# A gated feed-forward's down-projection: one engine's order stays written out, another's is handed to the scheduler

## The chip, the cores and the metric

The kernel runs on one core of a Trainium2 chip. Its five engines each take instructions from a queue of their own and keep its order: TensorE (PE) multiplies matrices into PSUM, VectorE (DVE) and ScalarE (ACT) work on tiles, GpSimd (POOL) does a little elementwise work and issues some stores, SyncE (SP) issues most DMAs. An instruction that waits for a semaphore holds back all that stands behind it on its engine. The metric is the device time of one launch in microseconds (us); times of a kernel are medians over its runs.

## The reference

One layer of a streaming encoder over 2048 prompt rows and 64 sample rows of width 1024. The last of its three sub-layers is the one that matters here:

```
def conv_ffn(xn, ff_buf, w_up, ffn_conv_w, w_down):
    up, ff_new = causal_dwconv(xn @ w_up, ff_buf, ffn_conv_w)
    a, g = jnp.split(up, 2, axis=-1)
    return (jax.nn.gelu(g) * a) @ w_down, ff_new
...
    y, ff_new = conv_ffn(rms_norm(x, p['norm_ffn_pre']), ff_buf, p['w_up'], p['ffn_conv_w'], p['w_down'])
    x = x + rms_norm(y, p['norm_ffn_post'])
```

`w_down` is 2816 by 1024, so the product sums over 22 blocks of 128. Everything is in float32, and the kernel splits each operand into a high and a low part and adds three products, so that the matrix engine keeps float32 accuracy.

## The kernel before, in words

Phases 1 to 3 do the token mixing and the cross-attention. Phase 4 (`phase4`) does the up-projection, the convolution and the gate, in three passes over the rows with 22 blocks each, and stores the gated rows, `da`, to the DRAM tile `hd` from POOL's queue (L1491 and after). Phase 5 (`phase5`) is the down-projection.

Phase 5 sums over the 22 blocks in six parts of 3, 3, 4, 4, 4 and 4 blocks (`PARTS`, L37). Each part goes through nine groups of rows: eight of 256 rows and one of the 64 sample rows (`groups`, `work`; the small group is last in part 0 and first in the others). In a list `work` of 54 items, item i is one part and one group:

- `load_down` loads a part's weights, 512 KB a block, into `raw` (three buffers, shared with phase 4's weights) and splits them: ACT casts the high part `dh` (L103), DVE subtracts to get the low part `dl` (L104). Two pools of weights alternate by part, so part p+2 overwrites those of part p.
- `load_h` loads a group's gated rows into `hr` (two buffers) and splits them the same way into the high and low half of `hh` (two buffers).
- For each 128 rows and each half of the 1024 columns, PE does three matmuls per block (L117 to L119; L128 and L129 for the small group) into a PSUM tile `y`, of which there are eight. In part 0 ACT copies it to the sum `acc`, later DVE adds it (L1589).
- In the last part `post` (L553) finishes each 128 rows: ACT squares (L560), POOL multiplies by the gain `gpost` (L564), DVE combines the statistics (L565, L95), POOL takes the power (L97), and `finish` (L570, DVE) multiplies and adds the residual row `xt` (two buffers). It then has SP store the two halves as `out_y`. `finish` of one tile is called within `post` of the next one.

What sets the order: PE and SP have been under a manual order since the start of phase 3 (L1058; the stack `self.ms` closes after phase 5), so on these two the instructions stand as the code issues them. In the last part ACT, DVE and POOL are under a manual order too (L1565). Elsewhere a scheduler places instructions. So SP issues a group's `hr` where `need(i + 1)` stands in the loop: one item ahead of the one being multiplied, and in the last part behind the `xt` loads and `out_y` stores of the items before it.

```
need(i)
need(i + 1)
...
h = hs.pop(i)
```

Of the kernel before, what the change touches and what calls it, by code (L numbers as in the profile page):

```python
# [35 lines left out]
HEAD = 120  # L36
PARTS = [3, 3, 4, 4, 4, 4]  # L37
# [4 lines left out]
def tw(j):  # L42
    return P if j < 16 else NS_TOK
# [24 lines left out]
class Prog:  # L68
# [68 lines left out]
    def build(self):  # L137
        tc, nc = self.tc, self.nc
        with ExitStack() as es:
            cp = self.pool(es, "const")  # L140

            self.pool(es, "edge", side="right").pool.tile([P, 8], F32, name="edge")
            self.rawp = self.pool(es, "raw", side="right")
            self.ident = cp.tile([P, P], F32, name="ident")
            make_identity(nc, self.ident)
            self.ones = cp.tile([P, P], F32, name="ones")
            nc.vector.memset(self.ones, 1.0)
            sm = cp.tile([P, 16 + 2 * NT], F32, name="small")
            self.mhalf, self.bg = sm[:, 0:8], sm[:, 8:16]
            self.r_all, self.rk_all = sm[:, 16:16 + NT], sm[:, 16 + NT:]  # L150
            nc.vector.memset(self.mhalf, -0.5)
            self.cst = cp.tile([P, CST_W], F32, name="cst")
            self.dma(self.cst, self.a["cst"])
            self.dma(self.bg, self.a["bg"].partition_broadcast(P))
            self.G = cp.tile([P, NT, 8], F32, name="G")
            self.aT = cp.tile([P, NR], F32, name="aT")
            self.em = cp.tile([P, NR], F32, name="em")
            self.wsb = cp.tile([P, NR], F32, name="wsb")
            self.wcb = cp.tile([P, NR], F32, name="wcb")
            dt = tc.dram_tile  # L160
            self.yaT = dt([4, P, T], F32, name="yaT")
            self.x2T = dt([KT, P, T], F32, name="x2Td")
            self.hd = dt([NF, P, T], F32, name="hd")
            self.wsd = dt([NF, P, 4, D // 2], F32, name="wsd")
            self.qT = dt([4, P, T], F32, name="qTd")
            self.kvo = dt([T, KVO], F32, name="kvo")
            self.nmd = dt([NR, P], F32, name="nmd")
            self.wd = dt([NR, P], F32, name="wd")
            self.mkd = dt([KT, P, NM], F32, name="mkd")
            self.mvd = dt([KT, P, NM], F32, name="mvd")  # L170
            self.od = dt([P, KT, NS_TOK], F32, name="od")
            self.ys = dt([NS_TOK, D], F32, name="ysd")
            self.x1 = dt([T, D], F32, name="x1d")
            self.x2 = dt([T, D], F32, name="x2d")
            self.pe = mybir.EngineType.PE
            self.zes = es.enter_context(ExitStack())
            self.qes = es.enter_context(ExitStack())
            self.fl_es = ExitStack()
            self.fl = self.pool(self.fl_es, "fill", space=PSUM)
            self.phase1()  # L180
            self.phase2()
            with ExitStack() as self.ms:
                self.phase3()
                self.phase4()
                self.phase5()


    def phase1(self):
# [1319 lines left out]
    def phase5(self):  # L1508
        tc, nc, a = self.tc, self.nc, self.a
        V = nc.vector  # L1510
        with ExitStack() as es:
            ac0 = self.pool(es, "p5a")
            w0 = self.pool(es, "p5w")
            ac1 = self.pool(es, "p5b")
# [8 lines left out]
            def load_down(pi, f0, nf):  # L1523
                ws = []
                pool = w1 if pi % 2 else w0
                for i in range(nf):
                    raw = self.raw(a["w_down"][f0 + i])
                    wh = pool.tile([P, D], F32R, tag="h%d" % i, name="dh", bufs=1)
                    wl = pool.tile([P, D], F32R, tag="l%d" % i, name="dl", bufs=1)
                    self.split(wh, wl, raw)  # L1530
                    ws.append((wh, wl))
                return ws

            def load_h(f0, nf, t0):
                n = min(2 * P, T - t0)
                hr = ld.tile([P, 4, 2 * P], F32, tag="hr", name="hr", bufs=2)
                self.dma(hr[:, :nf, :n], self.hd[f0:f0 + nf, :, t0:t0 + n].rearrange("f p t -> p f t"))
                hh = ld.tile([P, 2, 4, 2 * P], F32R, tag="hh", name="hh", bufs=2)
                if n == 2 * P:
                    self.split(hh[:, 0, :nf], hh[:, 1, :nf], hr[:, :nf])  # L1540
                    return hh
                h2 = hh[:, 0, :, 0:P].rearrange("p f (two t) -> p f two t", two=2)
                self.split(h2[:, :nf, 0], h2[:, :nf, 1], hr[:, :nf, :n])
                return h2

            groups = [NP_TOK] + list(range(0, NP_TOK, 2 * P))
            f0s = [sum(PARTS[:i]) for i in range(len(PARTS))]
# [3 lines left out]
            def need(i):  # L1551
                if i < len(work) and i not in hs:
                    pi, t0 = work[i]
                    hs[i] = load_h(f0s[pi], PARTS[pi], t0)
            with tc.high_priority(offset=HEAD):
                need(0)
                ws = {0: load_down(0, 0, PARTS[0])}
            held = None
            tail = None
            for i, (pi, t0) in enumerate(work):  # L1560
                last = pi == len(PARTS) - 1
                if i == len(PARTS):
                    self.dma(gpost, a["g_ffnpost"].partition_broadcast(P))
                if last and tail is None:
                    tail = es.enter_context(tc.manual_schedule(engines={mybir.EngineType.Activation,  # L1565
                                                                        mybir.EngineType.DVE, mybir.EngineType.Pool})) or 1
                need(i)
                need(i + 1)
                if t0 == groups[3] and pi + 1 < len(PARTS):
                    ws[pi + 1] = load_down(pi + 1, f0s[pi + 1], PARTS[pi + 1])  # L1570
                h = hs.pop(i)
                for j in range(t0 // P, (t0 + min(2 * P, T - t0) + P - 1) // P):
                    w = tw(j)
                    s = j * P - t0
                    if last:
                        xt = ld.tile([P, D], F32, tag="xt", name="xt5", bufs=2)
                        self.dma(xt[:w], self.x2[j * P:j * P + w])
                    for nh in range(2):
                        sl = slice(nh * 512, (nh + 1) * 512)
                        pt = py.tile([P, 512], F32, tag="y", name="y5")  # L1580
                        if w == P:
                            self.mm3(pt, [(h[:, 0, q, s:s + P], h[:, 1, q, s:s + P], wh[:, sl], wl[:, sl])
                                          for q, (wh, wl) in enumerate(ws[pi])])
                        else:
                            self.mm2(pt, [(h[:, q], wh[:, sl], wl[:, sl]) for q, (wh, wl) in enumerate(ws[pi])])
                        if pi == 0:
                            nc.scalar.copy(acc[j][:, sl], pt)
                        else:
                            V.tensor_tensor(out=acc[j][:, sl], in0=pt, in1=acc[j][:, sl], op=ALU.add)  # L1589
                    if last:  # L1590
                        yv = acc[j]
                        if w < P:
                            fo = ev.tile([P, D], F32, name="fo5")
                            self.fold(fo[:w], yv)
                            yv = fo
                        f = self.post(ev, [yv[:w, 0:512], yv[:w, 512:D]], gpost, xt, self.o["y"][j * P:j * P + w], w=w,
                                      yn=yv, junk=junk, hold=held or (), pg=j != 15)
                        held = [f]
                if i and work[i - 1][0] != pi:
                    ws.pop(pi - 1, None)  # L1600
# [89 lines left out]
```

## Time and profile before

| | us |
|---|---|
| median of 3 runs | 2946.56 |
| lowest and highest run | 2938.88, 2947.24 |
| the profiled execution's own time | 2947.28 |
| its span, first to last instruction | 2945.6 |

The rows below are from the profiled execution. Its time less its span is 1.7 us, which lies around the instructions. Times in rows are us from the span's start unless marked ns; phase 5's matmuls run from 2400 to the end. A row of a timeline merges equal instructions (x2), gives start and duration, and in brackets how long the engine had stood idle before it and what ended that.

### The profile page before, as it was taken

The page shows a single profiled execution, that of the slowest core. Times are in us where ns is not written, and L with a number is a line of the kernel's source. Part 1 is how long each engine was busy: PE and PEld are TensorE (multiplying, and loading weights), DVE is VectorE, ACT ScalarE, POOL GpSimd, SP SyncE. Part 2 cuts the span into 40 slices and gives each one's busy share as a digit, 9 for nine tenths or more (in the row PEclk, how much of TensorE's full clock was granted, in tenths as well). Part 3 has the DMA queues.
Part 4 walks back from the last instruction along what each step waited for, and adds up shares of the span by engine and source line. Part 5 has one row for each costly group of instructions (what it writes and reads, how often), then busy time and mean ns, then how long its engine had stood idle before and what let it go on. Part 6 is the DMA issues. An engine that isn't in the chain of part 4 may idle for free.

```text
span 2945.6 us, 41739 instructions
## 1 busy us (share of the span) xinstructions
PE 2846.5 (97%) x15906; PEld 2628.0 (89%) x15906; DVE 1716.3 (58%) x2815; ACT 1206.6 (41%) x2463; POOL 378.0 (13%) x608
## 2 busy tenths in 40 slices
PE   8999999999999999999979999999999989999987
PEld 8999999998988877788779999999999988888875
DVE  6413422355666555666477778877877753443457
ACT  5224223234344443223256566656666653110122
POOL 1111011112212202222100000000000000000034
PEclk9999999999999999999989999999999999999998
DMA  8434332158666335777455544554454532221235
GB/s 277 149 98 134 99 112 94 57 159 278 219 206 219 127 108 172 235 257 241 152 176 201 168 157 167 194 173 157 156 174 154 174 109 82 84 73 45 82 120 164
DMA packets 211498, 456.84 MB, mean 155 GB/s; under 512 B 25414, under 2 KB 113672, under 8 KB 211298
## 3 DMA queue, kind: packets, MB, share of 16 engines
q1 hardware_dynamic: 180418, 346.14, 37.2%
q0 software_dynamic: 28720, 100.17, 8.9%
q10 hardware_dynamic: 2160, 7.87, 1.0%
q8 instruction: 125, 2.05, 0.3%
q14 instruction: 75, 0.61, 0.1%
HBM read 345.56 MB, written 108.54 MB: 154 GB/s over the span
## 4 chain that ended last, share of the span: by engine, by line
PE 51%; DVE 6%; DMA 4%; issue 2%; ACT 1%; SPq 1%; POOL 0%; DVEq 0%; POOLq 0%; ACTq 0%
PE up L117 10%; PE up L119 10%; PE up L118 10%; PE y L118 4%; PE y L119 4%; PE y L117 4%; DMA sums<-in_w_up 2%; DVE acc L570 1%; PE yo L117 1%; PE yo L118 1%; PE yo L119 1%; DMA hr<-hd 1%; PE sc L119 1%; PE sc L117 1%; PE sc L118 1%
## 5 line engine op out<-in xcount | busy, mean ns | idle before, releaser
L117 PE MATMUL y<-dh,hh 128*128 128x512 f32 x704 | 278.9, 396 | 20.5 <-ACT hh L103 15.4
L119 PE MATMUL y<-dh,hh 128*128 128x512 f32 x704 | 278.7, 396 | 2.4 <-DVE hh L104 2.3
L118 PE MATMUL y<-dl,hh 128*128 128x512 f32 x704 | 277.7, 394 | 2.4 <-DVE dl L104 2.4
L117 PE MATMUL mm<-xs,wh 128*128 128x384 f32 (+2 forms) x768 | 249.0, 324 | 10.3 <-ACT xs L109 7.5
L119 PE MATMUL mm<-xs,wl 128*128 128x384 f32 (+2 forms) x768 | 248.7, 324 | 1.0 <-DVE wl L104 1.0
L118 PE MATMUL mm<-xs,wh 128*128 128x384 f32 (+2 forms) x768 | 248.8, 324 | 0.0
L1589 DVE TENSOR_TENSOR acc<-y,acc 128x512 f32<-128x512 f32 x170 | 115.7, 689 | 179.8 <-PE y L119 176.9
L117 PE MATMUL up<-B,wa 128*128 128x352 f32 x528 | 172.5, 327 | 8.8 <-ACT wa L103 8.8
L117 PEld LDWEIGHTS y<-dh,hh 128*128 128x128 f32 x704 | 134.7, 191 | 51.1 <-ACT hh L103 17.9
L117 PE MATMUL up<-T,wb 128*128 128x352 f32 x528 | 172.4, 326 | 3.7 <-ACT wb L103 2.6
L119 PE MATMUL up<-B,wa 128*128 128x352 f32 x528 | 170.3, 323 | 3.2 <-DVE wa L104 3.2
L117 PE MATMUL mmb<-bh,xs 128*128 128x384 f32 (+1 forms) x512 | 173.4, 339 | 0.0
L119 PE MATMUL mmb<-bh,xs 128*128 128x384 f32 (+1 forms) x512 | 172.5, 337 | 0.0
L118 PE MATMUL mmb<-bl,xs 128*128 128x384 f32 (+1 forms) x512 | 172.4, 337 | 0.0
L118 PE MATMUL up<-T,wb 128*128 128x352 f32 x528 | 170.3, 322 | 2.0 <-DVE T L104 2.0
L103 ACT CAST hh<-hr 128x1024 fp32r<-128x1024 f32 (+3 forms) x54 | 49.4, 914 | 297.5 <-PE y L119 248.8
L118 PE MATMUL up<-B,wa 128*128 128x352 f32 x528 | 170.7, 323 | 0.1
L119 PE MATMUL up<-T,wb 128*128 128x352 f32 x528 | 169.7, 321 | 0.5 <-DVE wb L104 0.5
L119 PEld LDWEIGHTS y<-dh,hh 128*128 128x128 f32 x704 | 134.5, 191 | 33.5 <-DVE hh L104 5.6
L118 PEld LDWEIGHTS y<-dl,hh 128*128 128x128 f32 x704 | 134.5, 191 | 31.1 <-DVE dl L104 3.1
L76 POOL DMA_DIRECT2D hd<-da x88 | 47.5, 541 | 851.1 <-DVE da L1491 822.8
L117 PEld LDWEIGHTS mm<-xs,wh 128*128 128x128 f32 x768 | 145.8, 190 | 10.7 <-ACT xs L109 7.5
(462 smaller groups left out, 7853.4 us busy)
## 6 DMA issues: line engine op xcount, KB each, us to landing
ws<-wsd SPq DMA_DIRECT2D x132, 512.0 KB, 4.3
raw<-in_w_up SPq DMA_DIRECT2D x66, 512.0 KB, 5.4
raw<-in_wA SPq DMA_DIRECT2D x47, 512.0 KB, 3.6
sums<-in_w_up SPq DMA_DIRECT2D x176, 128.0 KB, 4.1
wsd<-sums POOLq DMA_DIRECT2D x44, 512.0 KB, 4.2
wr<-in_w_up SPq DMA_DIRECT2D x66, 256.0 KB, 4.6
xt<-in_x SPq DMA_DIRECT2D x32, 512.0 KB, 4.4
hr<-hd SPq DMA_DIRECT2D x32, 512.0 KB, 3.9
```

Of the source, the lines that this page charges most:

```text
L76: self.nc.gpsimd.dma_start(out=out, in_=in_)
L103: nc.scalar.copy(hi, src)
L117: nc.tensor.matmul(out, lhsT=lh, rhs=rh, start=(first and i == 0), stop=False, skip_group_check=more)
L118: nc.tensor.matmul(out, lhsT=lh, rhs=rl, start=False, stop=False, skip_group_check=more)
L119: nc.tensor.matmul(out, lhsT=ll, rhs=rh, start=False, stop=(last and i == n - 1), skip_group_check=more)
L570: nc.vector.scalar_tensor_tensor(out=yn[:w, sl], in0=yn[:w, sl], scalar=r[:w, 0:1], in1=xt[:w, sl], op0=ALU.mult, op1=ALU.add)
L1589: V.tensor_tensor(out=acc[j][:, sl], in0=pt, in1=acc[j][:, sl], op=ALU.add)
```

## The change

Phase 5 moves out of the block whose end closes SP's and PE's manual order, and opens a manual order of its own for PE alone. SP's instructions in phase 5 are now placed by the scheduler. In the code the first part's weights are asked for before the first rows, and no longer at a raised priority; a later part's weights are asked for ahead of the two `need` calls of the same item instead of behind them.

```
@@ -182,7 +182,7 @@
             with ExitStack() as self.ms:
                 self.phase3()
                 self.phase4()
-                self.phase5()
+            self.phase5()
@@ -1509,6 +1509,7 @@
         with ExitStack() as es:
+            es.enter_context(tc.manual_schedule(engines={self.pe}))
             ac0 = self.pool(es, "p5a")
@@ -1552,13 +1553,14 @@
-            with tc.high_priority(offset=HEAD):
-                need(0)
-                ws = {0: load_down(0, 0, PARTS[0])}
+            ws = {0: load_down(0, 0, PARTS[0])}
+            need(0)
             held = None
             tail = None
             for i, (pi, t0) in enumerate(work):
                 last = pi == len(PARTS) - 1
+                if t0 == groups[3] and pi + 1 < len(PARTS):
+                    ws[pi + 1] = load_down(pi + 1, f0s[pi + 1], PARTS[pi + 1])
...
                 need(i)
                 need(i + 1)
-                if t0 == groups[3] and pi + 1 < len(PARTS):
-                    ws[pi + 1] = load_down(pi + 1, f0s[pi + 1], PARTS[pi + 1])
```

PE and POOL issue the same instructions in the same order as before; so do ACT and DVE in phase 4 and in the last part. Three places differ.

SP in the last part, before, from the first 256-row group's `hr` (named by its buffer number; `fo5` is the small group's output, `acc0` that of the first 128 rows):

```order
L73 DMA hr_25355<-hd_86 128x4x256
L73 DMA xt5_25360<-x2d_97 64x1024
L73 DMA hr_25395<-hd_86 128x4x256
L73 DMA xt5_25400<-x2d_97 128x1024
L73 DMA out_y<-fo5_25382 64x512 x2
L73 DMA xt5_25444<-x2d_97 128x1024
L73 DMA out_y<-acc0_22831 128x512 x2
L73 DMA hr_25488<-hd_86 128x4x256
```

The same stretch of SP now:

```order
L73 DMA hr_25358<-hd_86 128x4x256
L73 DMA hr_25398<-hd_86 128x4x256
L73 DMA hr_25491<-hd_86 128x4x256
L73 DMA hr_25584<-hd_86 128x4x256
L73 DMA out_y<-fo5_25385 64x512 x2
L73 DMA xt5_25447<-x2d_97 128x1024
L73 DMA out_y<-acc0_22834 128x512 x2
L73 DMA xt5_25496<-x2d_97 128x1024
L73 DMA hr_25677<-hd_86 128x4x256
```

The third group's rows stood behind the store of `acc0`, and now those of the third and fourth stand ahead of the part's first store, and the fifth's behind `acc0`: two groups further ahead.

SP where phase 4 ends, before (`ws` and `wr1` are phase 4's last weights, `raw<-in_w_down` the first weights of phase 5):

```order
L73 DMA raw_22442<-in_w_up 128x1024
L73 DMA ws_22444<-wsd_87 128x1024
L73 DMA ws_22446<-wsd_87 128x1024
L73 DMA wr1_22448<-in_w_up 128x512
L73 DMA hr_22850<-hd_86 128x3x256
L73 DMA raw_22855<-in_w_down 128x1024
L73 DMA raw_22861<-in_w_down 128x1024
L73 DMA raw_22867<-in_w_down 128x1024
```

And now:

```order
L73 DMA raw_22442<-in_w_up 128x1024
L73 DMA raw_22853<-in_w_down 128x1024
L73 DMA ws_22444<-wsd_87 128x1024
L73 DMA raw_22859<-in_w_down 128x1024
L73 DMA ws_22446<-wsd_87 128x1024
L73 DMA wr1_22448<-in_w_up 128x512
L73 DMA raw_22865<-in_w_down 128x1024
L73 DMA hr_22871<-hd_86 128x3x256
L73 DMA hr_22876<-hd_86 128x3x256
L73 DMA xt5_25363<-x2d_97 64x1024
L73 DMA gpost_22851<-in_g_ffnpost 128x1024
L73 DMA hr_22925<-hd_86 128x3x256
```

Two of the first weights now stand among phase 4's last ones, and a residual row and the gain stand ahead of the third group's rows.

DVE where part 2 gives way to part 3, before (`acc15` is the last 128 rows of part 2, `acc16` the small group of part 3, `hh` the split of the group that follows it):

```order
L1589 TENSOR_TENSOR acc15_22846<-y5_24251,acc15_22846 128x512
L1589 TENSOR_TENSOR acc15_22846<-y5_24265,acc15_22846 128x512
L104 TENSOR_TENSOR hh_24281<-hr_24279,hh_24281 128x1024
L1589 TENSOR_TENSOR acc16_22847<-y5_24284,acc16_22847 128x512
L1589 TENSOR_TENSOR acc16_22847<-y5_24294,acc16_22847 128x512
L104 TENSOR_TENSOR hh_24306<-hr_24304,hh_24306 128x1024
```

And now:

```order
L1589 TENSOR_TENSOR acc15_22849<-y5_24254,acc15_22849 128x512
L104 TENSOR_TENSOR dl_24432<-raw_24429,dh_24431 128x1024
L1589 TENSOR_TENSOR acc15_22849<-y5_24268,acc15_22849 128x512
L104 TENSOR_TENSOR dl_24438<-raw_24435,dh_24437 128x1024
L104 TENSOR_TENSOR hh_24284<-hr_24282,hh_24284 128x1024
L1589 TENSOR_TENSOR acc16_22850<-y5_24287,acc16_22850 128x512
L1589 TENSOR_TENSOR acc16_22850<-y5_24297,acc16_22850 128x512
L104 TENSOR_TENSOR dl_24444<-raw_24441,dh_24443 128x1024
L104 TENSOR_TENSOR dl_24450<-raw_24447,dh_24449 128x1024
L104 TENSOR_TENSOR hh_24309<-hr_24307,hh_24309 128x1024
```

The splits of part 4's weights, which stood some groups later, now stand around the change of parts, two of them ahead of the split that the next group needs.

## Rows read from the trace of the kernel before

**Rows 1.** The page: busy us of each engine, share of span, instructions.

```profile
PE 2846.5 (97%) x15906; PEld 2628.0 (89%) x15906; DVE 1716.3 (58%) x2815; ACT 1206.6 (41%) x2463; POOL 378.0 (13%) x608
```

**Rows 2.** Busy time by stretch: first parts of phase 5, two loops of the last.

```profile
core 0: us, PE busy (x) PEld busy (x) DVE busy (x) ACT busy (x) POOL busy (x), PEclk, DMA share, GB/s
2404.00:2818.00 414.00, 414.00 (x1816) 342.49 (x1817) 164.18 (x204) 78.59 (x98) 0.00 (x0) 0.99 0.25 76
...
2840.05:2856.14 16.09, 11.46 (x48) 8.86 (x48) 10.98 (x14) 3.94 (x9) 7.51 (x6) 1.00 0.51 163
2856.14:2872.30 16.16, 12.90 (x48) 9.68 (x48) 11.00 (x14) 3.94 (x9) 7.52 (x6) 0.89 0.52 163
```

**Rows 3.** Waits from 2811 on: total us, times, longest.

```profile
ACT hh L103 <- DMA hr<-hd: 39.6, 6, 6.8
...
PE y L117 <- ACT hh L103: 15.4, 6, 4.1
```

**Rows 4.** The chain that ended last, one loop of the last part: start, us, what.

```profile
2834.45 4.44 DMA hr<-hd
2838.97 1.06 ACT hh L103
2840.09 1.10 issue
2841.19 1.28 DVE acc L1589 x2
2842.47 2.36 DVE acc L570 x2
...
2850.20 4.79 DMA hr<-hd
```

**Rows 5.** Timeline of DVE in the last part.

```profile
2835.23 0.15 DVE L95 TENSOR_SCALAR pov<-poss 128x1 f32<-128x1 f32 x1
2840.05 1.22 DVE L104 TENSOR_TENSOR hh<-hr,hh 128x1024 fp32r<-128x1024 f32 x1 [4.66 <-ACT hh L103]
...
2920.30 1.23 DVE L104 TENSOR_TENSOR hh<-hr,hh 128x1024 fp32r<-128x1024 f32 x1 [4.93 <-ACT hh L103]
...
2931.25 1.28 DVE L1589 TENSOR_TENSOR acc<-y,acc 128x512 f32<-128x512 f32 x2
```

**Rows 6.** Timeline of SP's queue in the last part.

```profile
2848.07 2.04 SPq L73 DMA_DIRECT2D out_y<-acc  x2
2850.20 0.39 SPq L73 DMA_DIRECT2D hr<-hd  x1
...
2914.47 0.39 SPq L73 DMA_DIRECT2D hr<-hd  x1
```

**Rows 7.** The tile xt from 2820 on: issues, and issue to landing.

```profile
L73 SPq DMA_DIRECT2D xt<-x2d x15: 341/384/525, 2830.0 to 2935.3; - x15
...
DMA to landing us min/median/max: 3.6/3.8/5.6
```

**Rows 8.** Timeline where phase 5 starts: PE, then ACT, then DVE.

```profile
2400.62 0.80 PE L117 MATMUL y<-dh,hh 128*128 128x512 f32 x1 [5.12 <-ACT dh L103]
2403.76 0.80 PE L118 MATMUL y<-dl,hh 128*128 128x512 f32 x1 [2.35 <-DVE dl L104]
...
2399.52 2.94 ACT L103 CAST dh<-raw 128x1024 fp32r<-128x1024 f32 x3
...
2402.50 3.48 DVE L104 TENSOR_TENSOR dl<-raw,dh 128x1024 fp32r<-128x1024 f32 x3
```

**Rows 9.** Timeline of DVE where part 2 gives way to part 3.

```profile
2633.10 0.69 DVE L1589 TENSOR_TENSOR acc<-y,acc 128x512 f32<-128x512 f32 x1 [2.03 <-PE y L119]
2634.19 1.23 DVE L104 TENSOR_TENSOR hh<-hr,hh 128x1024 fp32r<-128x1024 f32 x1 [0.40 <-ACT hh L103]
...
2636.73 0.69 DVE L1589 TENSOR_TENSOR acc<-y,acc 128x512 f32<-128x512 f32 x1 [0.71 <-PE y L129]
```

**Rows 10.** Timeline of DVE and POOL at the first `post` of the last part.

```profile
2823.57 1.99 DVE L104 TENSOR_TENSOR hh<-hr,hh 128x1024 fp32r<-128x1024 f32 x1 [0.15 <-ACT hh L103]
...
2821.92 2.55 POOL L564 TENSOR_TENSOR fo<-fo,gpost 64x512 f32<-64x512 f32 x2 [418.85 <-ACT junk L560]
2824.44 1.55 POOL L97 TENSOR_TENSOR por<-pov,small 64x1 f32<-64x1 f32 x1
```

More of the change, by code (lines that the diff above doesn't have):

```diff
@@ L184, in build @@
                 self.phase4()
-                self.phase5()
+            self.phase5()
     def phase1(self):
@@ L1511, in phase5 @@
         with ExitStack() as es:
+            es.enter_context(tc.manual_schedule(engines={self.pe}))
             ac0 = self.pool(es, "p5a")
@@ L1554, in need @@
                     hs[i] = load_h(f0s[pi], PARTS[pi], t0)
-            with tc.high_priority(offset=HEAD):
-                need(0)
-                ws = {0: load_down(0, 0, PARTS[0])}
+            ws = {0: load_down(0, 0, PARTS[0])}
+            need(0)
             held = None
@@ L1561, in phase5 @@
                 last = pi == len(PARTS) - 1
+                if t0 == groups[3] and pi + 1 < len(PARTS):
+                    ws[pi + 1] = load_down(pi + 1, f0s[pi + 1], PARTS[pi + 1])
                 if i == len(PARTS):
@@ L1568, in phase5 @@
                 need(i + 1)
-                if t0 == groups[3] and pi + 1 < len(PARTS):
-                    ws[pi + 1] = load_down(pi + 1, f0s[pi + 1], PARTS[pi + 1])
                 h = hs.pop(i)
```

## The prediction, made before the changed kernel was run

> **What bounds the kernel now.** First the page's busy times: PE is busy for 97% of the span [rows 1], so only the stretches where PE waits can give much back. The busy times by stretch find them: through the first five parts of phase 5 PE is busy for all of 414.00 us, but a 16.1 us loop of the last part holds only 11.5 to 12.9 us of PE [rows 2]. The reader is to see three things there: PE idles, DVE is no fuller (11.0 of 16.1 us), and PE's granted clock in the second of these loops is 0.89, a mean of time at 2.4 GHz and some at 1.2 GHz, where the long stretch had 0.99. The table of waits then names the reason: PE waits for ACT's cast of the gated rows six times, and that cast waits for the load of `hr` six times, 39.6 us in all [rows 3].
>
> The chain of waits shows why the load is late [rows 4]. It goes round: load of `hr`, ACT's cast, DVE's subtraction (inside the "issue" step), DVE's adds and finishes of the group before, next load of `hr`. Two orders close this circle. On DVE the split of group g+1 stands ahead of the adds of group g. On SP the load of group g+2 stands behind the store of a tile of group g, and it starts where the two stores end [rows 6]. So the load of one group waits for DVE's finish, and the finish waits for the load of the group before. No engine is the bound in this part; the order on two queues is. One turn takes 16.0 us: the loads run from 2834.45 [rows 4] to 2914.47 [rows 6] with five turns between.
>
> **The change part by part.** *SP in the last part.* The third and fourth groups' rows now stand ahead of the first store, the fifth's behind the store of the first large tile, and so on, one group's rows per two tiles. Each load also needs its buffer, which is free when the group two before it has been split. Group g+4's load needs the split of group g+2, which DVE does before the adds of group g+1; the store behind that load belongs to a tile that DVE finishes after that split. So the new order on SP agrees with DVE's order and nothing has to go round. A load now has about two groups of time instead of none, against the 4.4 us that it takes.
>
> What is late next? DVE's own work. When it doesn't wait, its group lasts from 2920.30 (split) to 2931.25 (first add of the group after) [rows 5]: 10.95 us. PE's group is 4 PSUM tiles of 12 matmuls; at 414.00 us for 1816 matmuls [rows 2], 0.228 us each, that is 10.94 us (10.88 us at 0.2267, the rate without the slow first microseconds). The two are equal within 0.1 us, and PE enters the stretch ahead: it has a group in PSUM before DVE needs it, as the eight `y` tiles are two groups. I take 10.95 us.
>
> The sum: DVE is done with the first large group at 2835.23 plus 0.1; the split that now comes at 2840.05 [rows 5] moves there, 4.7 us earlier. From 2840.05 to 2920.30 there are five turns of 16.05 us; five of 10.95 us save 25.5 us. The last group, from 2931.25 on, never waited for a load and stays as it is. Together 30.2 us off.
>
> *Loads that share the DMAs.* A turn moves 163 GB/s by 16.1 us, 2.6 MB [rows 2]; in 10.95 us that is 240 GB/s, and the DMA share would go from 0.51 to 0.75. The nearest thing that can be late is `xt`, the residual row two tiles ahead: it is issued some 2.9 us after the finish that frees its buffer starts (two stores first), and used 10.95 us after that finish, so it may take 8.0 us. It takes 3.6 to 5.6 us now [rows 7]. At a 1.47 times denser traffic 5.6 would be 8.2 us, which costs 0.2 us in each of six groups, 1 us; with 3.8 us times 1.47 it costs nothing, which I take, since the median row is nearer.
>
> *SP where phase 4 ends.* Two weight loads of phase 5 now stand between phase 4's last loads. Their buffers were emptied before the ones that the loads behind them wait for, so SP loses the issue alone, 0.34 to 0.53 us each [rows 7], with the last unit of phase 4 still 10 us of matmuls away: nothing. PE's waits of 5.12 and 2.35 us at the start of phase 5 [rows 8] do not go either: they end with ACT's and DVE's split of the weights, which stand behind phase 4's last gate on both queues before and after. Bounds: 7.5 us gained if the weights came into use as they land, 1.0 us lost if the two issues came through to PE. I take 0, as the order on ACT and DVE there is the same to the instruction. The gain's load ahead of the third group's rows waits only for instructions of phase 4 that end before the split on which that load waits anyway.
>
> *Weights ahead of rows at each change of parts.* At the change from part 2 to 3 the last add starts at 2633.10 and PE, after the small group, takes the next large one when its second tile is out, about 2636.5 [rows 9]; the low half is first read two matmuls later, at 2637.0. Before, that split ended at 2635.4. Now the weight splits stand ahead of it. A weight split takes 1.16 us (3.48 us for three), a cast 0.98 (2.94 for three) [rows 8]. The first cast may start when PE is done with the block that it overwrites, nine matmuls or 2.05 us before the end of the part, so its split ends 0.1 us after 2633.10; add (0.7), split (1.16) and rows' split (1.23) end at 2636.3. That leaves 0.7 us. With three blocks in the part (1 to 2) the same count leaves about 0.3 us. Cost 0, with 0.5 us at each of four changes, 2 us, as the upper bound; below nothing it cannot go, as PE had no idle time there.
>
> *DVE beside POOL.* Next to a multiplication on POOL a split on DVE took 1.99 us instead of 1.22 us [rows 10, 5]; next to that split POOL's power took 1.55 us [rows 10]. In the closed-up loop the split follows at once on the part of `post` that POOL runs beside. In the chain of each tile POOL's multiplication has ended by then, and its power waits for DVE's last small operation (L95), right behind which the split starts; so the split goes first, and the power still ends before the finish that needs it, 2.4 us on (a split and two adds). I take 0. If instead each of the six splits met POOL first, as the one in the row did, it would take 0.77 us more, 4.6 us in all. The Trainium skill, "SBUF — State Buffer", section "Who interferes with whom", says that a DVE instruction with two inputs in SBUF and a GpSimd instruction that reads SBUF exclude each other for the whole instruction, and that the order of issue decides which one waits. The two long durations of the rows agree with it; by the rule each split of the new loop would either come first and cost nothing or lose what it lost there.
>
> The sum against the profiled execution: 2947.28 - 30.2 = 2917.1 us. The profile's execution lies 0.7 us above the median of the runs, which would make it 2916.4; with half a microsecond for the small costs I say 2917.
>
> **The rivals.**
>
> *PE becomes the bound at its lower rate.* For: the loops of the last part run at a granted clock of 0.89 and 12.9 us of PE per group [rows 2]. Then five turns save 3.15 us each and the first 4.7: 20.5 us, 2927 us. Against: the clock falls after idle time, in the stretch without idle time it is 0.99.
>
> *DMAs become the bound.* If a turn's 2.6 MB moved at 190 GB/s, a turn would take 13.8 us: 4.7 and five times 2.25 saved, 16 us, 2931 us. Against: the share of 0.75.
>
> *Splits beside POOL* lose the race of the paragraph above: 4.6 us back, 2922 us. For: the one row. Against: the order of the waits.
>
> *Slower: weights arrive one by one at the change of parts.* There are three raw buffers and four weights in a part, so the fourth load waits for the first's split, and it stands on SP ahead of the next rows. If loads of weights came into DVE's order ahead of rows that PE needs, each would cost a landing (4.4 us, as a load of the same size in rows 4), a cast and a split, 6.5 us. With two of them at each of four changes 52 us, less a cover of 0.7 us each, minus the 30.2 us: 2966 us. It decides from 7.6 us of PE idle per change on. Against: three of the four are loaded a part ahead, and the fourth's split stands behind the adds of the small group, when PE has a large group of 10.9 us in hand.
>
> *The change doesn't do what it says*, the rows are still loaded late: 2947 us. Against: the order on SP shows them ahead.
>
> **How the numbers follow.** Forecast 0.78, with its own range of 2911 to 2924 (the costs above on the upper side; on the lower the run-to-run spread of before, whose lowest run is 8 us under its median). PE's clock 0.05, DMAs 0.05, POOL 0.05, slower 0.04, no change 0.03. A measurement of this kernel tells 0.3%, 9 us, from no change. Faster by more than that: 0.78 + 0.05 + 0.05 + 0.05, less 0.01 for mishaps, 0.92; within it 0.04; slower 0.04. The range 2909 to 2930 takes in the forecast and two of the rivals, and leaves out the rest.
>
> **What would show it.** Right: in the last part no wait of ACT's cast for `hr`, splits on DVE 10.95 us apart, a granted clock of 1.0 to the last group, and the start of the last part where it was (2818). Wrong in a step: PE idle between 2480 and 2818 (change of parts); PE idle longer than 7.5 us at 2400; DVE's finish waiting for `xt`; splits of 2 us. The forecast as a whole is wrong if the turns stay near 16 us.

## The result, and the profile after

The changed kernel takes 2913.69 us (median of 4 runs, 2911.2 to 2917.14); the kernel before, run beside it, takes 2943.83 us (4 runs, 2938.88 to 2947.24). The ratio is 0.9900, 95% interval 0.9879 to 0.992: faster by 30.1 us. The prediction had 2917 us and a gain of 30.2 us. The 3 us between 2917 and 2913.69 are no step of it: its sum starts at one execution of 2947.28 us, and the kernel before has a median of 2943.83 us.

The profiled execution took 2911.2 us, with a span of 2909.5 us. That is 36.1 us less than the span before, and the gain proper is the smaller part that lies in phase 5: from its first matmul to the end of the span it was 2945.6 - 2400.62 = 544.98 us [rows 8], and now it is 2909.5 - 2394.85 = 514.65 us, 30.3 us less. The other 5.8 us arise before phase 5, where the change moves nothing but some of SP's loads. Nothing is to be read from them: phase 5 starts between 2394.1 and 2403.2 us in the four profiles of this study that keep SP's manual order through phase 5, and between 2391.4 and 2402.1 us in the four that end it before.

The page's busy times after the change; they answer to [rows 1]:

```profile
PE 2833.1 (97%) x15906; PEld 2621.9 (90%) x15906; DVE 1717.1 (59%) x2815; ACT 1204.8 (41%) x2463; POOL 383.8 (13%) x608
```

The instruction counts are the same, and DVE, the engine that sets the new turn, is as busy as before. PE's share stays at 97% while the kernel gets 1% faster, so this row would not have told anyone where the time was. The busy times by stretch do, as in [rows 2]:

```profile
core 0: us, PE busy (x) PEld busy (x) DVE busy (x) ACT busy (x) POOL busy (x), PEclk, DMA share, GB/s
2404.00:2818.00 414.00, 414.00 (x1827) 342.55 (x1826) 163.98 (x206) 79.94 (x103) 2.19 (x2) 1.00 0.24 71
...
2833.00:2844.00 11.00, 11.00 (x50) 9.09 (x50) 10.93 (x14) 3.83 (x9) 8.41 (x7) 1.00 0.78 241
2844.00:2855.00 11.00, 11.00 (x50) 9.13 (x49) 10.93 (x14) 3.84 (x9) 8.40 (x7) 1.00 0.74 241
```

The long stretch of the first five parts is full, as it was. In the last part a turn is 11.00 us instead of 16.1 us, DVE is busy for 10.93 us of it and PE for all of it, at a granted clock of 1.00. The same 14 DVE instructions as before fill the turn: the 5 us that went were waiting, not work.

The table of waits from 2805 us on, which answers to [rows 3] (total us, times, longest):

```profile
DVE acc L1589 <- PE y L119: 4.1, 2, 2.0
...
DVE hh L104 <- ACT hh L103: 0.6, 2, 0.4
```

The two rows of before, 39.6 us of ACT waiting for `hr` and 15.4 us of PE waiting for ACT, are gone. The chain that ended last no longer goes through a DMA; one turn of it, beside [rows 4]:

```profile
2862.31 1.01 issue
2863.32 1.28 DVE acc L1589 x2
2864.61 2.36 DVE acc L570 x2
2866.97 1.18 DVE poss L565
2868.24 1.28 DVE acc L1589 x2
2869.52 2.37 DVE acc L570 x2
2871.89 1.19 DVE poss L565
2873.31 1.01 issue
```

From "issue" to "issue" (inside which lies the split) it is 11.00 us, and every step is DVE's. DVE's timeline, beside [rows 5]:

```profile
2829.20 1.23 DVE L104 TENSOR_TENSOR hh<-hr,hh 128x1024 fp32r<-128x1024 f32 x1
...
2840.19 1.23 DVE L104 TENSOR_TENSOR hh<-hr,hh 128x1024 fp32r<-128x1024 f32 x1
...
2884.17 1.23 DVE L104 TENSOR_TENSOR hh<-hr,hh 128x1024 fp32r<-128x1024 f32 x1
```

The splits have no idle time before them (no bracket). Between the first and the last of these rows lie five turns, 54.97 us, 10.99 us each. SP's queue shows why, beside [rows 6]:

```profile
2826.24 2.04 SPq L73 DMA_DIRECT2D out_y<-acc  x2
2828.33 0.43 SPq L73 DMA_DIRECT2D xt<-x2d  x1
2830.45 0.38 SPq L73 DMA_DIRECT2D hr<-hd  x1
```

The load of `hr` now starts where the split that frees its buffer ends (2829.20 + 1.23 = 2830.43), and not where a store of the group before ends. Its rows are split two turns later.

### The profile page after: what moved, and what is told of

It reads as the page before. It is cut to its first block, busy times and chain, and to the rows that moved or that the text cites. A ratio compares the mean times of both kernels' runs of the same rounds, so it can differ in the third digit from the quotient of the medians.

```text
span 2909.5 us, 41745 instructions
## 1 busy us (share of the span) xinstructions
PE 2833.1 (97%) x15906; PEld 2621.9 (90%) x15906; DVE 1717.1 (59%) x2815; ACT 1204.8 (41%) x2463; POOL 383.8 (13%) x608
## 4 chain that ended last, share of the span: by engine, by line
PE 51%; DVE 7%; DMA 3%; issue 2%; ACT 1%; SPq 1%; POOL 0%; DVEq 0%; POOLq 0%; ACTq 0%
PE up L117 10%; PE up L119 10%; PE up L118 10%; PE y L118 5%; PE y L119 5%; PE y L117 4%; DMA sums<-in_w_up 2%; DVE acc L570 1%; PE yo L119 1%; PE yo L117 1%; PE yo L118 1%; PE sc L119 1%; PE sc L117 1%; PE sc L118 1%; DVE acc L1589 1%
## 5 line engine op out<-in xcount | busy, mean ns | idle before, releaser
L117 PE MATMUL y<-dh,hh 128*128 128x512 f32 x704 | 275.0, 391 | 5.1 <-ACT dh L103 5.1
L119 PE MATMUL y<-dh,hh 128*128 128x512 f32 x704 | 274.8, 390 | 0.0
```

The source lines that it names most:

```text
L117: nc.tensor.matmul(out, lhsT=lh, rhs=rh, start=(first and i == 0), stop=False, skip_group_check=more)
L119: nc.tensor.matmul(out, lhsT=ll, rhs=rh, start=False, stop=(last and i == n - 1), skip_group_check=more)
```

## Experiments: which part of the change does it

Two theories had to be told apart first. The circle theory, the prediction's own: the gain comes from SP issuing `hr` further ahead, and nothing else in the change matters. Its rival: the new order of the code does it (weights ahead of rows, no raised priority). The ratios compare with runs of the kernel before that were made beside each set: 2945.55 us (13 runs, 2942.5 to 2947.49) for all experiments but those with four buffers and with one buffer, and 2939.71 us (13 runs, 2934.34 to 2947.09) for these two.

**Only SP freed.** The code of phase 5 stays in the order of before, with the raised priority; the phase leaves the block of the manual order and gets one for PE:

```
                 self.phase4()
-                self.phase5()
+            self.phase5()
...
         with ExitStack() as es:
+            es.enter_context(tc.manual_schedule(engines={self.pe}))
```

> The kernel before with one half of the change: SyncE's manual order ends with the up-projection, TensorE keeps one; the code asks for rows and weights in the old order and with the old raised priority. Theory (the rows' loads of the last part move ahead of its stores): the whole gain, 30 us under before, turns of 11.0 us on VectorE in the last part. Rival (the gain comes from asking for weights ahead of rows): no gain, turns of 16 us, within 3 us of before.

Measured: 2914.28 us (4 runs, 2910.62 to 2919.3), ratio 0.9895 (0.988 to 0.991). Phase 5 takes 514.6 us in its profile, as in the changed kernel, and DVE's splits stand 11.0 us apart:

```profile
2832.04 1.22 DVE L104 TENSOR_TENSOR hh<-hr,hh 128x1024 fp32r<-128x1024 f32 x1
...
2843.04 1.23 DVE L104 TENSOR_TENSOR hh<-hr,hh 128x1024 fp32r<-128x1024 f32 x1
```

The whole gain comes with SP's order.

**Only the order of the code.** The other half: weights ahead of rows, no raised priority, SP still under the manual order.

```
-            with tc.high_priority(offset=HEAD):
-                need(0)
-                ws = {0: load_down(0, 0, PARTS[0])}
+            ws = {0: load_down(0, 0, PARTS[0])}
+            need(0)
...
+                if t0 == groups[3] and pi + 1 < len(PARTS):
+                    ws[pi + 1] = load_down(pi + 1, f0s[pi + 1], PARTS[pi + 1])
...
                 need(i)
                 need(i + 1)
-                if t0 == groups[3] and pi + 1 < len(PARTS):
-                    ws[pi + 1] = load_down(pi + 1, f0s[pi + 1], PARTS[pi + 1])
```

> The changed kernel with the other half alone: weights are asked for ahead of rows, without the raised priority, but SyncE stays under the manual order through the down-projection. Theory: no gain; the third group's load stands behind the first tile's store as before, turns of 16.0 us, within 3 us of before. Rival (weights ahead): 30 us under before.

Measured: 2945.9 us (10 runs, 2938.08 to 2949.66), ratio 0.9998 (0.9988 to 1.0008). The circle is still there: a wait of 39.1 us for `hr`, a load right behind two stores, and splits 15.7 to 16.1 us apart with idle time before them. The rows are from the waits, SP's queue and DVE's timeline of this kernel:

```profile
ACT hh L103 <- DMA hr<-hd: 39.1, 6, 6.7
```

```profile
2847.13 2.03 SPq L73 DMA_DIRECT2D out_y<-acc  x2
2849.25 0.39 SPq L73 DMA_DIRECT2D hr<-hd  x1
```

```profile
2839.10 1.23 DVE L104 TENSOR_TENSOR hh<-hr,hh 128x1024 fp32r<-128x1024 f32 x1 [4.98 <-ACT hh L103]
...
2854.86 1.22 DVE L104 TENSOR_TENSOR hh<-hr,hh 128x1024 fp32r<-128x1024 f32 x1 [4.70 <-ACT hh L103]
```

The code's new order gives nothing and costs nothing that this measurement resolves. The rival falls.

**One load moved by hand.** Freeing SP changes its order in many places. Here the kernel before keeps SP's manual order, and only the DMA of `hr` is issued one group earlier in the last part (`fetch` is the DMA out of `load_h`, whose split stays where it was):

```
                 need(i)
                 need(i + 1)
+                if last:
+                    fetch(i + 2)
```

> The kernel before with SyncE still under its manual order; in the last part alone the load of the rows is issued one group earlier by hand, so one load's place in SyncE's order differs and the later ones move up by one group. Theory: a load then has a whole group of 11 us against a landing of 4 to 5 us, so the turn falls to 11.0 us as in the changed kernel and the time to 30 us under before, with nothing else changed. Rival (the scheduler's freedom in all of the down-projection matters, weights included): less than half of it, under 15 us.

Measured: 2914.15 us (4 runs, 2909.7 to 2919.8), ratio 0.9895 (0.988 to 0.991); phase 5 takes 514.9 us. Its SP queue and its DVE timeline:

```profile
2845.85 2.04 SPq L73 DMA_DIRECT2D out_y<-acc  x2
2847.98 0.39 SPq L73 DMA_DIRECT2D hr<-hd  x1
2848.46 0.52 SPq L73 DMA_DIRECT2D xt<-x2d  x1
```

```profile
2848.82 1.23 DVE L104 TENSOR_TENSOR hh<-hr,hh 128x1024 fp32r<-128x1024 f32 x1
...
2859.81 1.23 DVE L104 TENSOR_TENSOR hh<-hr,hh 128x1024 fp32r<-128x1024 f32 x1
```

SP looks as it did before: the load goes out right behind the same two stores. But it carries the rows of the split at 2859.81, 11.8 us later, and no longer those of the split that DVE needs next. So the position behind a store does no harm by itself. The harm was that DVE's next instruction needed the load, and that the store ahead of the load needed what DVE had done just before. One group of distance opens the circle, and it gives the whole gain.

**Depth instead of place.** If loads came late for want of buffers, four of them would help. The order on SP is that of before, to the instruction:

```
-                hr = ld.tile([P, 4, 2 * P], F32, tag="hr", name="hr", bufs=2)
+                hr = ld.tile([P, 4, 2 * P], F32, tag="hr", name="hr", bufs=4)
```

> The kernel before with four buffers for the loaded rows instead of two; SyncE's order is the same instruction for instruction. Theory: the load waits for its place behind the store and for no buffer, so nothing changes: turns of 16.0 us, within 3 us of before. Rival (the depth of buffering is what the loads lack): turns of 11 us and 30 us under before.

Measured: 2938.91 us (10 runs, 2934.8 to 2946.98), ratio 0.9996 (0.9985 to 1.0008). Its waits:

```profile
ACT hh L103 <- DMA hr<-hd: 40.1, 6, 6.9
...
PE y L117 <- ACT hh L103: 16.6, 6, 4.3
```

Nothing moved: SP still starts a load of `hr` at 2844.26 us, right behind two stores (2842.14 us, 2.03 us long), and the splits stand 15.8 to 16.3 us apart. A buffer that is free is of no use to a load that stands in a queue behind a store.

**One buffer in the changed kernel.** The counterpart: `bufs=1` for `hr`, everything else as in the changed kernel.

```
-                hr = ld.tile([P, 4, 2 * P], F32, tag="hr", name="hr", bufs=2)
+                hr = ld.tile([P, 4, 2 * P], F32, tag="hr", name="hr", bufs=1)
```

> The changed kernel with one buffer for the loaded rows instead of two. Theory: a load may start when the split of the group before has ended, lands 4 to 5 us later and is wanted one turn of 11 us after that split, so one buffer is enough: turns of 11.0 us, within 3 us of the changed kernel. Rival (the two groups of lead that the new order has are needed): a wait of VectorE or ScalarE for the rows comes back and the gain of 30 us shrinks by more than 5 us.

Measured: 2909.79 us (4 runs, 2907.9 to 2914.07), ratio 0.9901 (0.9886 to 0.9916), the changed kernel's gain. The last part keeps its turn: five turns between splits take 54.97 us, as with two buffers. So one buffer is enough there, as the theory has it. Waits for the rows do come back, but in parts 0 and 1 alone (ACT waits twice for `hr`, 3.8 and 3.0 us), and the gain of 29.9 us has not shrunk by the 5 us of the rival.

What one buffer costs lies ahead of the last part. Phase 5 is 516.6 us long in this profile, 1.9 us more than with two. PE reaches the small group of part 0, 70 us after the start of phase 5, 0.8 us later than in the changed kernel (71.09 against 70.32 us after its first matmul), and that of part 2 1.9 us later (143.07 against 141.17 us). The first 0.8 us lie in the first 10 us, where PE's granted clock is 0.52 against 0.60 and PE does 17 matmuls instead of 20. Why is not shown; PE's waits there are the same. The other 1.1 us lie at the change from part 0 to part 1. There a second split of weights stands ahead of the rows' split on DVE, where the changed kernel has the rows' split first, and PE waits for it. DVE's timeline and then PE's:

```profile
2467.39 1.22 DVE L104 TENSOR_TENSOR dl<-raw,dh 128x1024 fp32r<-128x1024 f32 x1
2468.53 0.95 DVE L104 TENSOR_TENSOR hh<-hr,hh 128x768 fp32r<-128x768 f32 x1
```

```profile
2469.54 0.50 PE L119 MATMUL y<-dh,hh 128*128 128x512 f32 x1 [0.74 <-DVE hh L104]
```

So this edit changed the order on DVE too, outside the last part. The times of the runs do not resolve the 1.9 us.

**What bounds the new turn.** In the changed kernel's turn DVE (10.93 us busy of 11.00) and PE (full) are equal within the reading. In this kernel the gain's multiplication, which POOL does for all row tiles but the last, goes to DVE. That adds two instructions a tile to DVE and leaves POOL the power alone:

```
-                                      yn=yv, junk=junk, hold=held or (), pg=j != 15)
+                                      yn=yv, junk=junk, hold=held or (), pg=False)
```

> The changed kernel with the product with the gain moved from GpSimd to VectorE for all tiles (it is on VectorE for the last tile already). Theory: VectorE's turn falls from 11.0 to about 9.3 us (a tile of 4.06 us as the last one has: two adds 1.2, two finishes 1.3, two products 1.2, 0.3 for the statistics), since its finishes no longer wait beside GpSimd; but TensorE needs 10.9 us a group, so the turn stays at 10.9 and the end comes 1 us earlier at most, which the time cannot tell. Rival (VectorE alone bounds the last part): turns of 9.3 us and 8 to 10 us under the changed kernel.

Measured: 2914.76 us (4 runs, 2911.77 to 2916.74), ratio 0.9895 (0.988 to 0.991), the same as the changed kernel. Busy times by stretch (columns as above) and DVE's timeline of one turn:

```profile
2844.30:2855.18 10.88, 10.88 (x49) 9.01 (x48) 9.23 (x18) 3.83 (x9) 1.95 (x2) 1.00 0.79 241
```

```profile
2851.78 0.69 DVE L1589 TENSOR_TENSOR acc<-y,acc 128x512 f32<-128x512 f32 x1 [1.37 <-PE y L119]
2852.39 1.41 DVE L570 SCALAR_TENSOR_TENSOR acc<-acc,por,xt 128x512 f32<-128x512 f32 x2
2853.71 1.29 DVE L564 TENSOR_TENSOR acc<-acc,gpost 128x512 f32<-128x512 f32 x2
2854.91 0.15 DVE L565 TENSOR_TENSOR poss<-poss 128x1 f32<-128x1 f32 x1
```

DVE does four instructions more per turn and is busy 1.70 us less. Alone, its two finishes (L570) take 1.41 us and the sum of squares (L565) 0.15 us; beside POOL they take 2.44 and 1.25 us (below). DVE then waits for PE, the turn is PE's own 10.88 us, and phase 5 is 512.9 us long, 1.7 us shorter. None of that is PE's: its last matmul ends 504.1 us after its first in both kernels (2394.85 to 2898.95, and 2402.09 to 2906.14). The 1.7 us lie behind it. In the changed kernel DVE is late from the start of the last part: its first add of a large group starts at 2819.36 us, 2.0 us after PE's matmuls for these 128 rows end (2817.35 us). A turn that is 0.1 us longer than PE's cannot win this back; at the last 128 rows, behind which no split stands any more, 1.1 us are left. With the product on DVE the last add starts as soon as PE is done. The last add of the two kernels on DVE's timeline, the changed one first:

```profile
2900.05 1.28 DVE L1589 TENSOR_TENSOR acc<-y,acc 128x512 f32<-128x512 f32 x2
```

```profile
2906.18 0.69 DVE L1589 TENSOR_TENSOR acc<-y,acc 128x512 f32<-128x512 f32 x1 [1.36 <-PE y L119]
```

It ends 2.38 us after PE's last matmul in the one and 0.73 us in the other, which is the 1.7 us. The expectation had 1 us at most. The times of the runs do not show it. So the eight PSUM tiles hide a DVE that is slightly too slow from PE: PE has no wait in the last part in either kernel. What PE's waits leave to gain in phase 5 lies at its start.

## Why the prediction was right, step by step

**The circle on two queues.** Right, and shown by three runs: SP's order alone gives the gain, one load moved by one group gives it too, and more buffers do not.

**The new turn, and the sum.** DVE's own 10.95 us was forecast, 10.99 us came. PE's turn was 10.88 us, the lower of the two readings. PE is ahead, as forecast, but not by a whole group: its matmuls for 128 rows end 1.1 to 2.7 us before DVE's adds start, and that was enough. The split that now follows the first large group's was to come 4.7 us earlier: its distance to the split before it fell from 16.48 to 11.74 us, 4.74 us. Five turns were to save 25.5 us: they went from 80.25 us [rows 5] to 54.97 us, 25.28 us. From the last split to the end of the span it was 2945.6 - 2920.30 = 25.30 us and is 2909.5 - 2884.17 = 25.33 us, unchanged as forecast. Another 0.34 us came off between the start of phase 5 and the last part's first splits, from two steps that had been put at nothing (the entry and the changes of parts, below). 4.74 + 25.28 + 0.34 - 0.03 = 30.33 us.

**Shared DMAs.** The traffic came out as worked out, 241 GB/s forecast as 240, at a share of up to 0.78 forecast as 0.75. What it does to a transfer was the wrong way round: the bound took the landing of `xt` to grow by 1.47 with the density, and it fell, from a longest of 5.6 us [rows 7] to 4.0 us. From 2815 us on, for `xt`, in the changed kernel and then in the one with a load moved by hand:

```profile
DMA to landing us min/median/max: 3.6/3.6/4.0
```

```profile
DMA to landing us min/median/max: 3.6/3.9/5.7
```

The traces show what the long landings go with. In the kernel before, the `xt` loads that SP issues 0.5 us behind a load of `hr` took 5.4 to 5.6 us, the others 3.6 to 4.6 us. The first kind:

```profile
2850.20 0.39 SPq L73 DMA_DIRECT2D hr<-hd  x1
2850.67 0.51 SPq L73 DMA_DIRECT2D xt<-x2d  x1
```

In the changed kernel none of them stands right behind a load of `hr`. In the kernel with a load moved by hand some still do, and in the dense turns (239 to 241 GB/s) these take 5.4 to 5.7 us and the others 3.7 to 4.3 us. So the landing followed the load just ahead and not the mean traffic of a turn. No finish waits for `xt`. The value taken, nothing, was right; the reason for its upper bound was not.

**Entry of phase 5.** Nothing was forecast, against a possible gain of 7.5 us. PE's first two waits are those of [rows 8], 5.12 and 2.35 us:

```profile
2394.85 0.79 PE L117 MATMUL y<-dh,hh 128*128 128x512 f32 x1 [5.12 <-ACT dh L103]
2398.00 0.80 PE L118 MATMUL y<-dl,hh 128*128 128x512 f32 x1 [2.36 <-DVE dl L104]
```

The first weights are issued earlier and split no earlier, since the order on ACT and DVE there is the same: SP's queue starts with the three 9.3 us before phase 5's first matmul in the kernel before, and 51.5, 41.0 and 27.6 us before it in the changed one. Something was gained here all the same, 0.6 us: PE reaches the small group of part 0 70.32 us after its first matmul and not 70.89 us. It does 20 matmuls in the first 10 us and not 18, at a granted clock of 0.60 and not 0.54. Most other kernels fall into the same two groups, 70.2 to 70.3 us with SP freed and 70.8 to 71.0 us without; the one with one buffer does not (71.09 us). Why the clock rises sooner is open.

**Weights ahead of rows at the changes of parts.** Forecast to cost nothing, with 0.7 us to spare at the change from part 2 to 3. PE has no wait at any of the changes. Of the entry's gain 0.1 us is lost by the small group of part 2 and another 0.1 us by that of part 3, and no more behind it. DVE's timeline at the change from part 2 to 3, beside [rows 9]:

```profile
2626.03 1.23 DVE L104 TENSOR_TENSOR dl<-raw,dh 128x1024 fp32r<-128x1024 f32 x1 [1.07 <-ACT dh L103]
2627.17 0.68 DVE L1589 TENSOR_TENSOR acc<-y,acc 128x512 f32<-128x512 f32 x1
2627.77 1.22 DVE L104 TENSOR_TENSOR dl<-raw,dh 128x1024 fp32r<-128x1024 f32 x1
2628.91 1.22 DVE L104 TENSOR_TENSOR hh<-hr,hh 128x1024 fp32r<-128x1024 f32 x1
```

The rows' split ends at 2630.1, 3.0 us after the last add starts; 3.2 us had been worked out, of the 3.9 us there were. PE is busy for all of the 414.00 us around it. The slower rival (weights one by one, 2966 us) falls with that.

**DVE beside POOL.** Right on the order: the split comes first, lasts 1.23 us, and POOL's power is the one that is stretched, to 1.41 us when it meets a split and 0.54 us when it does not:

```profile
2829.42 1.41 POOL L97 TENSOR_TENSOR por<-pov,small 128x1 f32<-128x1 f32 x1 [0.35 <-DVE pov L95]
2831.93 3.22 POOL L564 TENSOR_TENSOR acc<-acc,gpost 128x512 f32<-128x512 f32 x2 [1.10 <-ACT junk L560]
2835.49 0.54 POOL L97 TENSOR_TENSOR por<-pov,small 128x1 f32<-128x1 f32 x1 [0.35 <-DVE pov L95]
```

It ends at 2830.83, before the finish that needs it at 2831.55. The rival of 4.6 us did not come.

**PE's clock.** The rival at the lower rate fell: the granted clock is 1.00 in the turns in which PE doesn't wait. The 0.89 of before stood in turns in which it did, and went with the waits.

## What to carry to other kernels

When no engine is full in a stretch, follow the chain of waits round once: a load that stands in an in-order queue behind a store closes a circle, if that store waits for work that another engine has queued behind the use of an earlier load. Move the load one step ahead in its queue before adding buffers: one step of distance gave 30 us here, two more buffers gave nothing. The busy share of the fullest engine hid this stretch at 97% before and after; only busy times by stretch showed it. The Trainium skill, "Perfetto Trace Analysis", section "Optimization Strategy", says that the most contended engine can change from regime to regime and that its gaps are to be traced to the semaphore waited for; the traces agree, with the addition that in this regime (11.5 us of PE and 11.0 us of DVE in a turn of 16.1 us) the bound was no engine at all.

## What the runs showed that was not expected

A stretch that the change hardly touches moves from profile to profile by more than a third of this gain: phase 5 starts between 2391.4 and 2403.2 us in the eight profiles, and by 9 us even among the three in which SP's order ahead of it is the same too (the kernel before, one load moved, four buffers). Two single profiles can be compared only from a common point on, here phase 5's first matmul.

DVE pays for POOL's company in small instructions too. In the changed kernel's turn, the sum of squares over 128x1 takes 1.25 us, until POOL's multiplication (L564, 2831.93 + 3.22 above) is done, and the two finishes 2.44 us:

```profile
2831.55 2.44 DVE L570 SCALAR_TENSOR_TENSOR acc<-acc,por,xt 128x512 f32<-128x512 f32 x2
2833.91 1.25 DVE L565 TENSOR_TENSOR poss<-poss 128x1 f32<-128x1 f32 x1
```

The Trainium skill, "SBUF — State Buffer", section "Who interferes with whom", has a DVE instruction with two inputs in SBUF and a GpSimd instruction that reads SBUF exclude each other for a whole instruction; the rows agree, down to one of 128x1. With POOL relieved of the product, DVE did four instructions more per turn in 1.70 us less. A product given to POOL to spare DVE cost DVE more than it saved; here the times of the runs don't show it, because PE is just as full.
